# A decoder layer on one core: every product and difference of two tensors moved from GpSimd to VectorE

## The chip, the cores and the metric

The kernel runs on 1 core of one Trainium2 chip. The metric is device time in microseconds (us) of one execution, lower is better. The engines are named as in the profile: PE is TensorE (matmuls), DVE is VectorE, ACT is ScalarE, POOL is GpSimd, and SP issues most of the transfers. Each engine works through its own queue of instructions in order.

## The reference

One layer over 1024 tokens of width 1024, all in float32:

```python
x = x + 0.5 * swiglu(rmsnorm(x, g1), w_gate1, w_up1, w_down1)      # hidden width 2816
h = rmsnorm(x, g_mix)
qa, ka, va, qkv_b, beta, decay, gdn_gate, gate_a, gate_b = split(h @ w_in)
# branch A: rotary on qa and ka, causal dilated window attention in 3 groups of 4 heads (64 wide),
#           groups merged by a softmax over their log-denominators
# branch B: short causal convolution and silu on q, k, v; gated DeltaNet in chunks,
#           8 heads of 128; rmsnorm of the result times silu(gdn_gate)
x = x + (sigmoid(gate_a) * (A @ w_branch_a) + sigmoid(gate_b) * (B @ w_branch_b)) @ w_out
x = x + 0.5 * swiglu(rmsnorm(x, g2), w_gate2, w_up2, w_down2)
return rmsnorm(x, g_final)

def rmsnorm(x, g):  return x * rsqrt(mean(x * x) + 1e-6) * g
def rope(x1, x2):   return concat(x1 * cos - x2 * sin, x2 * cos + x1 * sin)
```

## The kernel before

Every large float32 product is made of three matmuls on parts of its operands. An operand is split in two: the high part `fH` is a cast that ACT makes, and the low part `fL` is the difference between the operand and `fH`. For weights this is `ff_split`, on 128x512 pieces of the raw tile `fraw` that SP's queue loads. Its difference (L222) runs on DVE, except in the mixer, where the flag `C.pool_split` sends it to POOL. Three matmuls per step of 128 then go to PE (L161 for projections of the mixer and merge, L279 and L409 in the hidden layers, L589 in the down projections).

The program has these stages. (1) Norm of the eight input tiles and the first matmuls. (2) The hidden layer of the first feed-forward part and its down projection, at whose end `done1` makes the norm for the mixer, tile by tile; `First` then makes the values of the first attention group and PE's banks for them are copied out by ACT (L809). (3) The mixer, first attention: for each of six pairs of heads, two rotary tiles (`rope_tile`) and eight blocks. (4) The mixer, eight DeltaNet heads: `gdn_keys`, `gdn_inverse` (a triangular solve of 62 short dependent DVE steps, L1041 to L1047, then a merge on PE), `gdn_values`, `gdn_scan` (eight steps in which PE and DVE take turns; `R` L1192, `v` L1200). Projections of later heads and of the gates fill PE in between. (5) The merge of the branches with the next norm, (6) the second feed-forward part, and `done2` with the final norm.

The norm of a tile is in `make_h`: the square sum on ACT (L186), the reciprocal root on DVE in 12 small steps (`rsqrt_cols`, L123 to L130), the product with the gain, transposes on PE (L206) and a split of the result. On even input tiles DVE makes one instruction of gain and root (L196). On all other tiles POOL multiplies with the gain (L198) and ACT scales by the root (L200). `done2` does the same on POOL (L1493), with half of the scaling on ACT (L1495) and half on DVE (L1497).

In `rope_tile`, ACT's queue issues four transfers that swap the halves of a tile (L836); then DVE multiplies the tile with the cosine (L837), POOL the swapped one with the sine (L838), and DVE adds (L840, L845 or L848). In `gdn_keys`, POOL scales the keys by a factor per token (L1139).

The order on each engine is made by a list scheduler that goes by priorities. Inside the mixer each piece of code stands in a `band`: attention first, then head 0, head 1 and so on, and the projections (`bulk`, with their weight splits) last. A change of the engine of an instruction thus changes the order around it too. The weight ring holds nine `fH` and nine `fL` pieces and two raw tiles.

Of the kernel before, what the change touches and what calls it, by code (L numbers as in the profile page):

```python
# [133 lines left out]
def load_w(C, *parts):  # L134

    nc = C.nc
    raw = C.wp.tile([P, 2048], F32, name="fraw", tag="fraw", bufs=2)
    for view, src in parts:
        nc.sync.dma_start(view(raw), src)
    return [ff_split(C, raw[:, q * 512:q * 512 + 512], eng=nc.gpsimd if C.pool_split else None) for q in range(2)]  # L140


def load_w2(C, src):
# [43 lines left out]
    return rsqrt_cols(C, ssq, 1.0 / D, EPS, 1, "rn")[0]  # L187


def make_h(C, x_t, t, gB, pool, bufs, on_dve=False):  # L190

    nc = C.nc
    xs = row(C, pool, "xg", "xg", bufs)
    if on_dve:
        r = rstd(C, x_t, pool)
        nc.vector.scalar_tensor_tensor(xs, x_t, r, gB, op0=ALU.mult, op1=ALU.mult)  # L196
    else:
        nc.gpsimd.tensor_tensor(out=xs, in0=x_t, in1=gB, op=ALU.mult)  # L198
        r = rstd(C, x_t, pool)
        nc.scalar.activation(xs, xs, AF.Copy, scale=r)  # L200

    def turn():
        for q in range(2):
            ps = psum(C, "tA")
            for f in range(4):
                nc.tensor.transpose(ps[:, f * P:f * P + P], xs[:, (q * 4 + f) * P:(q * 4 + f) * P + P], C.ident)  # L206
            v = ps.rearrange("p (f t) -> p f t", t=P)
            split_to(C, C.hH[:, q * 4:q * 4 + 4, t * P:t * P + P], C.hL[:, q * 4:q * 4 + 4, t * P:t * P + P], v)

    return turn  # L210


def ff_split(C, src, n=512, eng=None):

    nc = C.nc
    H = C.wp.tile([P, 512], F32R, name="fH", tag="fH", bufs=9)
    L = C.wp.tile([P, 512], F32R, name="fL", tag="fL", bufs=9)
    h, l = H[:, :n], L[:, :n]
    if len(src.shape) == 3:
        h, l = [v.rearrange("p (k n) -> p k n", n=src.shape[2]) for v in (h, l)]  # L220
    nc.scalar.copy(h, src)  # L221
    (eng or nc.vector).tensor_tensor(out=l, in0=src, in1=h.bitcast(F32), op=ALU.subtract)  # L222
    return H, L


# [599 lines left out]
def rope_tile(C, w_in, c0, g):  # L825

    nc = C.nc
    raw, sw, out = t4(C, "xp")[:, :T], t4(C, "vb")[:, :T], t4(C, "ka")[:, :T]
    with band(C, "bulk"):
        W = load_w2(C, cols(w_in, c0))  # L830
        for a in (0, 1):
            ps = proj(C, W, a, "mm")
            nc.scalar.copy(raw[:, a * 512:a * 512 + 512], ps)
    with band(C, "att"):
        for b in range(4):
            nc.scalar.dma_start(sw[b * 32:b * 32 + 32, :], raw[(b ^ 1) * 32:(b ^ 1) * 32 + 32, :])  # L836
        nc.vector.tensor_tensor(out=raw, in0=raw, in1=C.cosT, op=ALU.mult)  # L837
        nc.gpsimd.tensor_tensor(out=sw, in0=sw, in1=C.sinT, op=ALU.mult)  # L838
        if g == 0:
            nc.vector.tensor_tensor(out=out, in0=raw, in1=sw, op=ALU.add)  # L840
        elif g == 1:
            for n in range(2):
                o = out.rearrange("p (r n i) -> p r n i", r=4, n=2)[:, :, n]
                a, b = [v[:, n * 512:n * 512 + 512].rearrange("p (i r) -> p r i", r=4) for v in (raw, sw)]
                nc.vector.tensor_tensor(out=o, in0=a, in1=b, op=ALU.add)  # L845
        else:
            a, b = [v.rearrange("p (i r) -> p r i", r=8) for v in (raw, sw)]
            nc.vector.tensor_tensor(out=out.rearrange("p (r i) -> p r i", r=8), in0=a, in1=b, op=ALU.add)  # L848
    return out
# [253 lines left out]
def gdn_keys(C, w_in, h, Dm):  # L1103

    nc = C.nc
    X = Head()
    X.h = h
    with band(C, f"h{h}"):
        ssq = C.gd.tile([P, 16], F32, name="gssq", tag="gssq", bufs=2)
        X.k = t4c(C, "ka")  # L1110
        gdn_conv(C, w_in, C_KB + h * P, 8 + h, X.k)
        X.kd = t4c(C, "ka")
        ssq_tokens(C, X.k, X.kd, ssq[:, 0:8])
        X.q = t4c(C, "ka")
        gdn_conv(C, w_in, C_QB + h * P, h, X.q)
        ssq_tokens(C, X.q, None, ssq[:, 8:16])
        rs, sv = rsqrt_cols(C, ssq, 1.0, EPS, 16, "rg")
        cl = C.gd.tile([P, 5, NT], F32, name="cl", tag="cl", bufs=2)
        s, X.nk, ks, X.so = cl[:, 0], cl[:, 1], cl[:, 2], cl[:, 3]
        ns = cl[:, 4]  # L1120
        nc.vector.tensor_tensor(out=s, in0=rs[:, 0:8], in1=rs[:, 0:8], op=ALU.mult)
        nc.vector.tensor_tensor(out=s, in0=s, in1=C.beta[:, :, h], op=ALU.mult)
        nc.vector.tensor_tensor(out=X.nk, in0=rs[:, 0:8], in1=sv[:, 0:8], op=ALU.mult)
        nc.vector.tensor_tensor(out=ks, in0=s, in1=C.eS[:, :, h], op=ALU.mult)
        nc.vector.tensor_scalar(X.so, rs[:, 8:16], float(P) ** -0.5, None, op0=ALU.mult)
        nc.vector.tensor_scalar(ns, s, -1.0, None, op0=ALU.mult)

        X.N, X.A = t4c(C, "ka"), t4c(C, "ka")
        for src, dst, sc in ((X.k, X.N, ns), (X.q, X.A, s)):
            for q in range(2):  # L1130
                ps = psum(C, "tA")
                for i in range(4):
                    c = q * 4 + i
                    nc.tensor.matmul(ps[:, i * P:i * P + P], X.k[:, c, :], src[:, c, :], start=True, stop=True)
                for i in range(4):
                    c = q * 4 + i
                    nc.vector.scalar_tensor_tensor(dst[:, c, :], ps[:, i * P:i * P + P], sc[:, c:c + 1], Dm[:, c, :],
                                                   op0=ALU.mult, op1=ALU.mult)
        nc.gpsimd.tensor_tensor(out=X.kd, in0=X.kd, in1=ks.unsqueeze(2).to_broadcast([P, NT, P]), op=ALU.mult)  # L1139
    return X  # L1140


# [262 lines left out]
def open_pools(C, tc, st):  # L1405
    C.nc = tc.nc
    C.tc = tc
    C.pool_split = False
    C.fx = None
    C.cp = st.enter_context(tc.tile_pool(name="cp", bufs=1))  # L1410
    C.hp = st.enter_context(tc.tile_pool(name="hp", bufs=1, reuse_waits="tile"))
    C.tp = st.enter_context(tc.tile_pool(name="tp", bufs=2))
    C.pp = st.enter_context(tc.tile_pool(name="pp", bufs=1, space=bass.MemoryType.PSUM))
    C.dp = st.enter_context(tc.tile_pool(name="dp", bufs=1, space=bass.MemoryType.DRAM))
    C.hH, C.hL = Quarters(), Quarters()
    for th in (0, 1):
        new_h(C, th)
    C.x1d = C.dp.tile([T, D], F32, name="x1d")
    C.x2d = C.dp.tile([T, D], F32, name="x2d")
    C.hd = {n: [C.dp.tile([P, 512], F32, name=f"hd{n}x{p}") for p in range(NPAIR)] for n in range(1, 8)}  # L1420
    C.od = [C.dp.tile([T, 2, 132], F32, name=f"od{g}") for g in range(3)]
    C.vd = [C.dp.tile([T, 256], F32, name=f"vd{g}") for g in (1, 2)]
    C.v0d = C.dp.tile([T, 272], F32, name="v0d")
    C.yad = C.dp.tile([P, 2, T], F32, name="yad")
    C.sgad = [C.dp.tile([P, T], F32, name=f"sgad{f}") for f in range(8)]
    C.sgbd = [C.dp.tile([P, T], F32, name=f"sgbd{f}") for f in range(8)]
    C.ybd = [C.dp.tile([P, T], F32, name=f"ybd{f}") for f in range(8)]
    C.nbd = [C.dp.tile([32, 1024], F32, name=f"nbd{f}") for f in range(2)]
    C.ud = [C.dp.tile([32, 1024], F32, name=f"ud{f}") for f in range(2)]


def layer(tc, I, out):
# [6 lines left out]
    with ExitStack() as st:  # L1439
# [3 lines left out]
        with pool("s1") as sp:  # L1443
# [4 lines left out]
            for t in range(NT):  # L1448
                if t:
                    nc.sync.dma_start(xs[t], I["x"][t * P:t * P + P])  # L1450
                make_h(C, xs[t], t, gB, sp, 8, t % 2 == 0)()
                if t == 1:
                    W = [ff_tiles(C, I[w], 0) for w in ("ffn1_w_gate", "ffn1_w_up")]
        with pool("fx") as C.fx:
# [22 lines left out]
            first.blocks(range(4, NT))  # L1477
        C.fx = None
        with pool("ms") as C.ms:
            C.pool_split = True  # L1480
            mixer(C, tc, I)
            C.pool_split = False
        with pool("fx2") as C.fx:
            gB2 = load_gain(C, I["ffn2_norm"])
            first = merge_out(C, tc, I, gB2)
# [4 lines left out]

            def done2(t, x):
                y = row(C, C.fx, "y", None, None)
                nc.gpsimd.tensor_tensor(out=y, in0=x, in1=gF, op=ALU.mult)  # L1493
                r = rstd(C, x, C.fx)
                nc.scalar.activation(y[:, :512], y[:, :512], AF.Copy, scale=r)  # L1495
                nc.sync.dma_start(out[t * P:t * P + P, :512], y[:, :512])
                nc.vector.tensor_scalar(y[:, 512:], y[:, 512:], r, None, op0=ALU.mult)  # L1497
                nc.sync.dma_start(out[t * P:t * P + P, 512:], y[:, 512:])

            ff_down(C, C.x2d, down, done2)  # L1500

# [25 lines left out]
```

## Time and profile before

| | |
|---|---|
| time, median of 3 runs | 2700.59 us (2696.6 to 2703.91) |
| time of the profiled execution | 2714.74 us |
| its span | 2713.0 us |
| busy PE, DVE, ACT, POOL | 2576.8, 1793.9, 1003.0, 317.8 us |
| POOL's products and differences | splits 173.7, rotary 34.6, norms 20.0 + 19.9 + 19.4 + 11.4, keys 15.2 us |
| granted PE clock, mean | 0.969 |

In rows of groups the columns are line, engine, operation, output and inputs, shapes, count, then busy time in us and mean of one in ns, then the idle time of the engine before them and what ended it. In a timeline, a row has the start and the length in us. In a list of waits, the first is who waited, behind the arrow who was waited for, then us in total, times, and the longest.

### The profile page before, as it was taken

The numbers are of one execution on the slowest core, as the hardware profiler recorded it, in microseconds if no ns is written. First come the engines' busy times: TensorE is split into PE (matmuls) and PEld (weight loads), VectorE is DVE, ScalarE is ACT, GpSimd is POOL, SyncE is SP. The second block draws the span as 40 slices with busy tenths as digits, with TensorE's granted clock in tenths as the row PEclk, the third lists the DMA queues.
The fourth block names the chain that finished last, engine by engine and source line by source line (L and its number), as shares of the span: only waits on it lengthen the run. The fifth ranks groups of instructions, "written<-read, shape, count | busy, mean of one in ns | idle before, by whom it ended". The sixth has DMA issues, their size and how long they took to land.

```text
span 2713.0 us, 35365 instructions
## 1 busy us (share of the span) xinstructions
PE 2576.8 (95%) x12739; PEld 2111.5 (78%) x12739; DVE 1793.9 (66%) x3923; ACT 1003.0 (37%) x1857; POOL 317.8 (12%) x236
## 2 busy tenths in 40 slices
PE   7999999999899999899999999899999999999996
PEld 6888888887777867777777777777778888888885
DVE  8866666678342335878787875635647866667677
ACT  5333333445332324423333333225434333333444
POOL 1000000002322232212122211200101000000002
PEclk9999999999988989999999998999999999999998
DMA  4322337553423222312112211225442332238452
GB/s 156 109 91 107 105 113 258 162 176 132 126 58 82 80 75 69 102 53 61 46 44 68 57 49 47 74 103 200 169 160 89 106 109 103 100 110 289 132 190 78
DMA packets 258174, 301.07 MB, mean 111 GB/s; under 512 B 41840, under 2 KB 175184, under 8 KB 258000
## 3 DMA queue, kind: packets, MB, share of 16 engines
q1 hardware_dynamic: 255696, 292.54, 32.9%
q10 hardware_dynamic: 2304, 6.29, 1.0%
q8 instruction: 100, 1.64, 0.2%
q14 instruction: 74, 0.61, 0.1%
HBM read 217.34 MB, written 75.14 MB: 108 GB/s over the span
## 4 chain that ended last, share of the span: by engine, by line
PE 43%; DVE 13%; DMA 1%; ACT 1%; issue 1%; SPq 0%; ACTq 0%; DVEq 0%
PE mm L161 10%; PE tC L409 6%; PE mm L409 4%; PE tM L409 4%; DVE fsP L1046 2%; PE mm L589 2%; PE tC L589 2%; PE tM L589 2%; PE tA L589 2%; PE tC L1386 2%; DVE fsP L1041 1%; PE mm L1386 1%; PE tC L161 1%; DVE fsT L1047 1%; DVE ka L970 1%
## 5 line engine op out<-in xcount | busy, mean ns | idle before, releaser
L221 ACT CAST fH<-fraw 128x512 fp32r<-128x512 f32 x482 | 295.2, 620 | 650.9 <-PE mm L161 190.6
L161 PE MATMUL mm<-hH,fL 128*128 128x512 f32 x1024 | 422.8, 413 | 0.0
L161 PE MATMUL mm<-hH,fH 128*128 128x512 f32 x1024 | 419.5, 410 | 0.0
L161 PE MATMUL mm<-hL,fH 128*128 128x512 f32 x1024 | 419.3, 409 | 0.0
L222 DVE TENSOR_TENSOR fL<-fraw,fH 128x512 fp32r<-128x512 f32 x354 | 246.4, 700 | 103.8 <-ACT fH L221 102.8
L222 POOL TENSOR_TENSOR fL<-fraw,fH 128x512 fp32r<-128x512 f32 x128 | 173.7, 1360 | 589.2 <-ACT fH L221 494.2
L161 PEld LDWEIGHTS mm<-hH,fL 128*128 128x128 f32 x1024 | 199.4, 195 | 37.5 <-issue 1.3
L161 PEld LDWEIGHTS mm<-hL,fH 128*128 128x128 f32 x1024 | 198.6, 194 | 38.0 <-issue 2.3
L161 PEld LDWEIGHTS mm<-hH,fH 128*128 128x128 f32 x1024 | 198.5, 194 | 37.0 <-issue 1.9
L409 PE MATMUL mm<-hH,fH 128*128 128x512 f32 x320 | 124.5, 389 | 0.0
L409 PE MATMUL mm<-hL,fH 128*128 128x512 f32 x320 | 124.5, 389 | 0.0
L409 PE MATMUL mm<-hH,fL 128*128 128x512 f32 x320 | 124.5, 389 | 0.0
L582 DVE TENSOR_TENSOR hid<-hid,fH 128x512 fp32r<-128x512 f32 x154 | 106.3, 691 | 4.8 <-ACT fH L581 4.8
L581 ACT CAST fH<-hid 128x512 fp32r<-128x512 f32 x154 | 94.8, 616 | 18.2 <-PE tM L409 6.6
L1493 POOL TENSOR_TENSOR y<-acc,gB 128x1024 f32<-128x1024 f32 x8 | 19.4, 2439 | 630.6 <-DVE acc L624 624.0
L970 DVE SCALAR_TENSOR_TENSOR ka<-xp,cw,ka 128x512 f32<-128x512 f32 x96 | 82.1, 857 | 15.4 <-ACT ka L968 13.9
L198 POOL TENSOR_TENSOR xg<-acc,gB 128x1024 f32<-128x1024 f32 x8 | 19.9, 2506 | 616.1 <-DVE acc L624 610.5
L221 ACT CAST fH<-hH 128x512 fp32r<-128x512 f32 x68 | 42.4, 623 | 101.9 <-PE tC L589 50.3
L222 DVE TENSOR_TENSOR fL<-hH,fH 128x512 fp32r<-128x512 f32 x68 | 49.1, 722 | 46.8 <-ACT fH L221 46.8
L589 PE MATMUL mm<-fL,fH 128*128 128x512 f32 x176 | 69.7, 396 | 4.5 <-DVE fL L222 4.5
L837 DVE TENSOR_TENSOR xp<-xp,U 128x1024 f32<-128x1024 f32 x12 | 17.0, 1420 | 82.8 <-DMA vb<-xp 82.8
L409 PEld LDWEIGHTS mm<-hL,fH 128*128 128x128 f32 x320 | 60.1, 188 | 12.6
(401 smaller groups left out, 6393.3 us busy)
## 6 DMA issues: line engine op xcount, KB each, us to landing
fraw<-in_w_in_dram SPq DMA_DIRECT2D x66, 512.0 KB, 3.7
fraw<-in_ffn_w_gate_dram SPq DMA_DIRECT2D x22, 1024.0 KB, 5.1
fraw<-in_ffn_w_up_dram SPq DMA_DIRECT2D x22, 1024.0 KB, 5.4
hL<-in_ffn_w_down_dram SPq DMA_DIRECT2D x8, 1024.0 KB, 6.6
fraw<-in_ffn_w_down_dram SPq DMA_DIRECT2D x8, 1024.0 KB, 6.3
fraw<-in_w_branch_b_dram SPq DMA_DIRECT2D x8, 1024.0 KB, 5.1
fraw<-in_w_out_dram SPq DMA_DIRECT2D x8, 1024.0 KB, 7.8
vb<-xp ACTq DMA_DIRECT2D x48, 128.0 KB, 2.4
```

The source lines that it names most:

```text
L161: nc.tensor.matmul(ps, w, x, start=k == 0 and i == 0, stop=k == kt - 1 and i == 2)
L221: nc.scalar.copy(h, src)
L222: (eng or nc.vector).tensor_tensor(out=l, in0=src, in1=h.bitcast(F32), op=ALU.subtract)
L409: nc.tensor.matmul(ps, w, x, start=opens and k == 0 and q == 0, stop=k == 3 and q == 2, skip_group_check=True)
L581: C.nc.scalar.copy(h, v.bitcast(F32))
L582: C.nc.vector.tensor_tensor(out=v, in0=v.bitcast(F32), in1=h.bitcast(F32), op=ALU.subtract)
L589: self.C.nc.tensor.matmul(ps, x[:, m], w, start=p == 0 and i == 0, stop=p == NPAIR - 1 and i == 2)
L970: nc.vector.scalar_tensor_tensor(o, x, w, o, op0=ALU.mult, op1=ALU.add)
L1041: nc.vector.tensor_tensor(out=v, in0=Th[:, :, :, 0:n], in1=mv, op=ALU.mult)
L1046: nc.vector.tensor_tensor(out=v, in0=Tx[:, 0:4, 0:n], in1=mv, op=ALU.mult)
L1047: nc.vector.tensor_reduce(out=Tx[:, 0:4, i], in_=v, axis=AX.X, op=ALU.add)
L1386: nc.tensor.matmul(ps, mx[:, c], W[k][w], start=i == 0, stop=i == len(seq) - 1)
```

## The change

All of POOL's operations on two tensors go to DVE. `ff_split` has no choice of engine any more; the second rotary product and the key scaling change their engine alone; and the norms use one DVE instruction for gain and root on every tile, so that ACT's scaling goes away too. In `done2` this instruction runs on two halves of the tile, each stored when it is done. POOL keeps memsets, one copy and the masking of the decay.

```diff
 def load_w(C, *parts):
-    return [ff_split(C, raw[:, q * 512:q * 512 + 512], eng=nc.gpsimd if C.pool_split else None) for q in range(2)]
+    return [ff_split(C, raw[:, q * 512:q * 512 + 512]) for q in range(2)]

-def make_h(C, x_t, t, gB, pool, bufs, on_dve=False):
+def make_h(C, x_t, t, gB, pool, bufs):
     xs = row(C, pool, "xg", "xg", bufs)
-    if on_dve:
-        r = rstd(C, x_t, pool)
-        nc.vector.scalar_tensor_tensor(xs, x_t, r, gB, op0=ALU.mult, op1=ALU.mult)
-    else:
-        nc.gpsimd.tensor_tensor(out=xs, in0=x_t, in1=gB, op=ALU.mult)
-        r = rstd(C, x_t, pool)
-        nc.scalar.activation(xs, xs, AF.Copy, scale=r)
+    r = rstd(C, x_t, pool)
+    nc.vector.scalar_tensor_tensor(xs, x_t, r, gB, op0=ALU.mult, op1=ALU.mult)

 def ff_split(...):
     nc.scalar.copy(h, src)
-    (eng or nc.vector).tensor_tensor(out=l, in0=src, in1=h.bitcast(F32), op=ALU.subtract)
+    nc.vector.tensor_tensor(out=l, in0=src, in1=h.bitcast(F32), op=ALU.subtract)

 def rope_tile(...):
-        nc.gpsimd.tensor_tensor(out=sw, in0=sw, in1=C.sinT, op=ALU.mult)
+        nc.vector.tensor_tensor(out=sw, in0=sw, in1=C.sinT, op=ALU.mult)

 def gdn_keys(...):
-        nc.gpsimd.tensor_tensor(out=X.kd, in0=X.kd, in1=ks.unsqueeze(2).to_broadcast([P, NT, P]), op=ALU.mult)
+        nc.vector.tensor_tensor(out=X.kd, in0=X.kd, in1=ks.unsqueeze(2).to_broadcast([P, NT, P]), op=ALU.mult)

 def done2(t, x):
-                nc.gpsimd.tensor_tensor(out=y, in0=x, in1=gF, op=ALU.mult)
                 r = rstd(C, x, C.fx)
-                nc.scalar.activation(y[:, :512], y[:, :512], AF.Copy, scale=r)
-                nc.sync.dma_start(out[t * P:t * P + P, :512], y[:, :512])
-                nc.vector.tensor_scalar(y[:, 512:], y[:, 512:], r, None, op0=ALU.mult)
-                nc.sync.dma_start(out[t * P:t * P + P, 512:], y[:, 512:])
+                for h in (slice(0, 512), slice(512, 1024)):
+                    nc.vector.scalar_tensor_tensor(y[:, h], x[:, h], r, gF[:, h], op0=ALU.mult, op1=ALU.mult)
+                    nc.sync.dma_start(out[t * P:t * P + P, h], y[:, h])
```

Lines of the changed kernel are a few less: the split L222 is L217 there, the solve's L1041 and L1042 are L1036 and L1037, the key scaling L1139 is L1134, ACT's copy L809 is L804.

Three places of the new order. First DVE's queue inside the triangular solve of the fifth head. `fsP` and `fsT` are the solve's, `seg` a part of the next head's decay, `vT` a convolution, `vb` the head's values. Before:

```order
L1041 TENSOR_TENSOR fsP<-fsT,Tm 128x104
L996 TENSOR_TENSOR seg<-masks,gH 128x512
L1042 TENSOR_REDUCE fsT<-fsP 128x2x4
L996 TENSOR_TENSOR seg<-masks,gL 128x512
L1041 TENSOR_TENSOR fsP<-fsT,Tm 128x112
```

and now, some steps earlier in the same solve:

```order
L1155 TENSOR_TENSOR vb<-tA,cl 128x512
L1036 TENSOR_TENSOR fsP<-fsT,Tm 128x24
L217 TENSOR_TENSOR fL<-fraw,fH 128x512
L1037 TENSOR_REDUCE fsT<-fsP 128x2x4
L965 SCALAR_TENSOR_TENSOR vT<-xp,cw,vT 128x512
L1036 TENSOR_TENSOR fsP<-fsT,Tm 128x32
```

Work of other parts stood between a product of the solve and its sum already; now splits stand there too. This solve has five of them, where it had none; two more stand between its end and the step that takes its result (`Tm`), one right behind that step, and two at the end of the scan.

Second, DVE's queue in the scan of the same head. `R`, `v`, `S` are the scan's, `cl` are the factors of the next head's keys, and `ka` in L1137 (now L1132) its key products. Before:

```order
L1122 TENSOR_TENSOR cl<-cl,beta 128x8
L1125 TENSOR_SCALAR cl<-rgy 128x8
L1124 TENSOR_TENSOR cl<-cl,ex 128x8
L1126 TENSOR_SCALAR cl<-cl 128x8
L1192 SCALAR_TENSOR_TENSOR R<-tC,neG,vb 128x128
L1137 SCALAR_TENSOR_TENSOR ka<-tA,cl,Dm 128x128 x2
L1200 COPY v_13337<-tC 128x128
```

and now:

```order
L1117 TENSOR_TENSOR cl<-cl,beta 128x8
L1119 TENSOR_TENSOR cl<-cl,ex 128x8
L1121 TENSOR_SCALAR cl<-cl 128x8
L1134 TENSOR_TENSOR ka<-ka,cl 128x1024
L1195 COPY v_13268<-tC 128x128
L1132 SCALAR_TENSOR_TENSOR ka<-tA,cl,Dm 128x128 x2
L1203 SCALAR_TENSOR_TENSOR S<-S,ex,tC 128x128
```

The key scaling (L1134) stands between the `R` and the `v` of one scan step, with the factors; it was on POOL.

Third, ACT's queue at the end of the first down projection. `sq` is the square sum of a finished tile `acc`, `xg` the normalised tile, `rny` its root from DVE, `vs` the copy of a bank that PE needs again. Before (with the buffers' numbers):

```order
L186 ACTIVATE sq_5836,ssq_5837<-acc_4856 128x1024
L221 CAST fH_6287<-fraw_6281 128x512
L200 ACTIVATE xg_5799<-xg_5799,rny_5805 128x1024
L809 COPY vs_5880<-tM_5855 128x272
L221 CAST fH_6559<-fraw_6557 128x512
L200 ACTIVATE xg_5834<-xg_5834,rny_5840 128x1024
```

and now:

```order
L186 ACTIVATE sq_5790,ssq_5791<-acc_4850 128x1024
L804 COPY vs_5868<-tM_5843 128x272
L216 CAST fH_6547<-fraw_6545 128x512
L216 CAST fH_6551<-fraw_6545 128x512
L804 COPY vs_5896<-tM_5871 128x272
L186 ACTIVATE sq_5824,ssq_5825<-acc_4852 128x1024
```

ACT's copy of the bank no longer stands behind scalings that wait for DVE's root; it stands behind square sums, which wait for finished tiles.

More of the change, by code (lines that the diff above doesn't have):

```diff
@@ L210, in make_h, with ff_split @@
     return turn
-def ff_split(C, src, n=512, eng=None):
+def ff_split(C, src, n=512):
     nc = C.nc
@@ L1407, in open_pools @@
     C.tc = tc
-    C.pool_split = False
     C.fx = None
@@ L1450, in layer @@
                     nc.sync.dma_start(xs[t], I["x"][t * P:t * P + P])
-                make_h(C, xs[t], t, gB, sp, 8, t % 2 == 0)()
+                make_h(C, xs[t], t, gB, sp, 8)()
                 if t == 1:
@@ L1479, in layer @@
         with pool("ms") as C.ms:
-            C.pool_split = True
             mixer(C, tc, I)
-            C.pool_split = False
         with pool("fx2") as C.fx:
```

## The prediction

> **What bounds the kernel now.** I read the page's costliest groups first, then the busy time by stage, then the timeline of VectorE (DVE) beside GpSimd (POOL), and last what TensorE (PE) waited for. The two groups that the change is mostly about, from the page:
>
> ```profile
> L222 DVE TENSOR_TENSOR fL<-fraw,fH 128x512 fp32r<-128x512 f32 x354 | 246.4, 700 | 103.8 <-ACT fH L221 102.8
> L222 POOL TENSOR_TENSOR fL<-fraw,fH 128x512 fp32r<-128x512 f32 x128 | 173.7, 1360 | 589.2 <-ACT fH L221 494.2
> ```
>
> One split of a weight tile costs 0.70 us on DVE and 1.36 on POOL, which is idle most of the time. By that alone the change loads the busier engine. The stages (columns: stretch, its length, then busy time and instruction count of PE, PE's weight loads, DVE, ACT, POOL, then granted clock, DMA share, GB/s):
>
> ```profile
> 0.00:50.00 50.00, 33.43 (x238) 31.69 (x239) 38.56 (x128) 30.52 (x49) 11.58 (x8) 0.97 0.53 191
> 600.00:715.00 115.00, 102.07 (x546) 88.89 (x545) 85.19 (x180) 57.19 (x99) 32.14 (x18) 0.94 0.38 124
> 715.00:1080.00 365.00, 346.79 (x1819) 274.89 (x1818) 138.56 (x391) 123.75 (x359) 92.53 (x60) 0.93 0.30 81
> 1080.00:1800.00 720.00, 669.65 (x3867) 539.36 (x3867) 538.84 (x1519) 241.12 (x426) 142.08 (x134) 0.95 0.22 60
> ...
> 2650.00:2713.00 63.00, 41.93 (x172) 33.82 (x170) 48.00 (x136) 26.15 (x45) 19.40 (x8) 0.86 0.21 77
> ```
>
> POOL works in five places: the first norm (0 to 50), the end of the first feed-forward part (600 to 715), attention (715 to 1080), the DeltaNet heads (1080 to 1800), and merge and final norm. In the hidden parts PE is always busy and POOL idle, so nothing happens there. In the heads DVE is busy 75% of the time with serial work, and PE follows it.
>
> What decides is what POOL does to DVE. From the timeline of the end (start, length, engine):
>
> ```profile
> 2692.73 2.40 POOL L1493 TENSOR_TENSOR y<-acc,gB 128x1024 f32<-128x1024 f32 x1 [1.17 <-DVE rny L130]
> 2692.86 2.29 DVE L129 SCALAR_TENSOR_TENSOR rnt<-rnt,rnv 128x1 f32<-128x1 f32 x1
> ```
>
> An operation on one element per partition lasts 2.29 us and ends with the POOL product that started just before it. The line's own view (min/median/max) of a sister operation, and a DVE group in one head that reads one operand from PSUM:
>
> ```profile
> L126 DVE CUSTOM_DVE_ANT_0 rny<-rny,magic x32: 145/159/2365, 6.4 to 2707.0; 128x2 uint16<-128x2 uint16 x32
> L1137 DVE SCALAR_TENSOR_TENSOR ka<-tA,cl,Dm 128x128 f32<-128x128 f32 x16 | 4.9, 342 | 0.0
> ```
>
> 0.16 is the normal price, 2.37 the price under a POOL product; the L1137 group keeps to 0.34. So POOL's products of two tensors stop DVE instructions that read two tensors from SBUF. [...]
>
> **The change part by part.** DVE gains 128 splits at 0.70 (90 us; 9 stand before 715, 40 in attention, 79 in the heads), 12 rotary and 8 key products at 1.23 (25), 20 norm products at 1.28 (26), and eight output tiles in two halves. POOL loses all of its products, ACT 20 scalings by the root and 8 of the output. What that does is different in each stage.
>
> *Start.* The rows of DVE and PE, and the price of the norm product on DVE:
>
> ```profile
> 17.29 2.11 DVE L222 TENSOR_TENSOR fL<-fraw,fH 128x512 fp32r<-128x512 f32 x1
> 19.92 6.84 DVE L222 TENSOR_TENSOR fL<-fraw,fH 128x512 fp32r<-128x512 f32 x5
> 25.02 0.39 PE L279 MATMUL tC<-hH,fL 128*128 128x256 f32 x1 [3.16 <-DVE fL L222]
> L196 DVE SCALAR_TENSOR_TENSOR xg<-xin,rny,gB x4: 1276/1278/1284, 8.3 to 39.6; 128x1024 f32<-128x1024 f32 x4
> ```
>
> Six splits took 8.95 us where 6 x 0.70 = 4.2 are due, and PE waited 3.16 for them. DVE pays 4 x 1.28 = 5.1 for the products of the odd tiles, mostly later, while PE has matmuls queued. I take -3 (ends: 0, if those products come in front of the splits, and -5).
>
> *End of the first down projection.* Here POOL, DVE and ACT stand in one chain:
>
> ```profile
> 638.92 2.90 DVE L222 TENSOR_TENSOR fL<-hH,fH 128x512 fp32r<-128x512 f32 x1
> ...
> PE tA L206 <- ACT xg L200: 4.3, 1, 4.3
> PE tM L806 <- ACT vs L809: 7.8, 1, 7.8
> ...
> 687.47 1.15 ACT L200 ACTIVATE xg<-xg,rny 128x1024 f32<-128x1024 f32 x1 [3.69 <-DVE rnv L123]
> ```
>
> The first wait is for the first normalised tile, whose root was held up on DVE by POOL. In the second PE needs a bank that ACT should have copied out; ACT stood at L200, waiting for the root. The change takes L200 out of ACT's queue and the stretches out of DVE's: both waits go, -12. The products that DVE takes over (8 x 1.28) are shorter than what POOL costs it there; late next is the first tile's square and root. Ends: -4, if DVE's own queue is late by as much, and -16, with the slow matmuls after each wait.
>
> *Attention.* Rotary: both products wait for the same transfer; POOL's is the longer one (first two rows), and PE waits for the sum (window 715 to 1080):
>
> ```profile
> L838 POOL TENSOR_TENSOR vb<-vb,Tm x12: 2355/2866/3442, 736.8 to 1013.2; 128x1024 f32<-128x1024 f32 x12
> L837 DVE TENSOR_TENSOR xp<-xp,U x12: 1215/1226/2104, 734.5 to 1013.2; 128x1024 f32<-128x1024 f32 x12
> ...
> PE tC L869 <- DVE ka L845: 5.1, 2, 4.3
> PE tC L869 <- DVE ka L848: 4.8, 1, 4.8
> PE tC L869 <- DVE ka L840: 2.7, 2, 2.6
> ```
>
> Before, the sum starts 2.87 after the transfer, now 2 x 1.23 = 2.45 if both products come after it. A split that stands ahead on POOL (1.36) no longer delays the product, and nothing stops the sum: 0.4 + 1.36 = 1.8 at best. I take 1.6 for each of the five waits: -8 (ends 0 and all 12.6). The 40 splits cost 28 us on an engine that is idle for 226 of 365: nothing, as long as each finds its ACT copy made.
>
> *Heads.* The DVE groups of one head (window 1440 to 1527), stretched ones with unstretched neighbours:
>
> ```profile
> L970 DVE SCALAR_TENSOR_TENSOR ka<-xp,cw,ka 128x512 f32<-128x512 f32 x12 | 9.9, 824 | 3.1 <-ACT ka L968 2.9
> L970 DVE SCALAR_TENSOR_TENSOR vT<-xp,cw,vT 128x512 f32<-128x512 f32 x6 | 4.5, 748 | 2.5 <-ACT vT L968 2.5
> L1041 DVE TENSOR_TENSOR fsP<-fsT,Tm 128x128 f32<-128x128 f32 x1 | 1.5, 1517 | 0.0
> L1046 DVE TENSOR_TENSOR fsP<-fsT,Tm 128x124 f32<-128x124 f32 x1 | 1.4, 1356 | 0.0
> L125 DVE TENSOR_SCALAR roy<-rov 128x8 int32<-128x8 int32 x1 | 1.1, 1105 | 0.0
> L1046 DVE TENSOR_TENSOR fsP<-fsT,Tm 128x76 f32<-128x76 f32 x1 | 1.1, 1093 | 0.0
> L1041 DVE TENSOR_TENSOR fsP<-fsT,Tm 128x16 f32<-128x16 f32 x1 | 1.1, 1081 | 0.0
> L1046 DVE TENSOR_TENSOR fsP<-fsT,Tm 128x128 f32<-128x128 f32 x1 | 0.4, 399 | 0.0
> L1041 DVE TENSOR_TENSOR fsP<-fsT,Tm 128x24 f32<-128x24 f32 x1 | 0.2, 189 | 0.0
> ```
>
> The four stretched steps of the triangular solve lose 1.12 + 0.96 + 0.69 + 0.89 = 3.7 against 0.40, 0.40, 0.40 and 0.19; the convolution 12 x 0.076 = 0.9, the root 0.9: 5.5 us a head, all on DVE's serial path. Into it come 79/8, about 10 splits (7.0) and the key product (1.2): 8.2. In the new order five splits stand inside the solve, where DVE waits for nothing: paid, 3.5. The key product stands in the scan between two steps that PE waits for: paid, 1.2. The other five stand where DVE has waits anyway:
>
> ```profile
> DVE vT L970 <- ACT vT L968: 5.0, 2, 2.5
> ...
> DVE ka L970 <- ACT ka L968: 2.9, 2, 2.3
> ```
>
> So 4.7 - 5.5 = -0.8 a head, -6 for eight. Ends: none paid, -44; all paid, and each split waiting for ACT's copy as the 354 on DVE do now (103.8/354 = 0.29), 8.2 + 2.9 - 5.5 = +5.6 a head, +45. I take a value near the middle, since the order shows half of the splits on each side. Queued behind a split that waits are the solve and the scan, and PE behind them. The weight loads wait on SP's queue for the splits to free the raw tile:
>
> ```profile
> SPq L139 <- POOL fL L222: 382.7, 54, 27.2
> ```
>
> They run far ahead of PE, so an earlier release by half a microsecond costs and gains nothing.
>
> *Merge and end.* One stretch stands in front of the second half's gates; at the end PE waits once for a split behind stretched operations, and two stretches follow its last matmul:
>
> ```profile
> 1952.66 2.36 DVE L129 SCALAR_TENSOR_TENSOR rnt<-rnt,rnv 128x1 f32<-128x1 f32 x1
> ...
> 2671.88 0.80 PE L589 MATMUL mm<-fL,fH 128*128 128x512 f32 x1 [4.49 <-DVE fL L222]
> ...
> 2698.05 2.20 DVE L128 TENSOR_TENSOR rnt<-rny 128x1 f32<-128x1 f32 x1
> ...
> 2703.15 2.20 DVE L128 TENSOR_TENSOR rnt<-rny 128x1 f32<-128x1 f32 x1
> ```
>
> Merge: -2 (0 to -6). End: PE's wait of 4.49 goes, and after the last matmul the two stretches of 2.2. Each of the last three tiles pays half a product (1.28/2 = 0.64) more on DVE: -4.5 - 4.4 + 1.9 = -7 (ends -2 and -9).
>
> Sum: -3 - 12 - 8 - 6 - 2 - 7 = -38. The profiled execution's span is 2713.0, its time 2714.74, 14 above the median of the runs shown, 2700.59; the profiled 2714.74 would become 2677, the median 2663.
>
> **The rivals.** *DVE becomes the bound in the heads, and the kernel slower.* For it: DVE 538.84 of 720 there, 8.2 us more a head, in-order waits for ACT. Against: the stretches go, and DVE still has waits to fill. At +45 in the heads the sum is 2700.6 - 32 + 45 = 2714; it turns to slower when a head loses more than 4 us. [...]
> *About no change:* the heads lose some 4 us each and eat the rest, 2700.
> *Hidden gain:* attention and heads give nothing, since PE's projections fill what comes free; start, projection, merge and end stay: -24, 2677.
> *None of the splits is paid:* heads -44, in all -76, 2625.
>
> **How the numbers follow.** Forecast (2640 to 2690) 0.48, hidden gain 0.20, none paid 0.14, no change 0.08, slower 0.10. A change under 0.3% (8 us) can't be told from none. Faster 0.48 + 0.20 + 0.14 = 0.82, same 0.08, slower 0.10. The range runs from the case that nothing is paid to that of no change, 2622 to 2698; slower and the tails stay out.
>
> **What would show it.** No 128x1 operation on DVE over 1 us; PE without the waits of 4.3, 7.8, 3.16 and 4.49; solve steps of 0.2 to 0.4 with splits of 0.7 between them; POOL busy under 30 us. I am wrong if DVE stands before L217 for ACT's copies by more than 0.4 us each in the heads, or if the new order leaves PE short of projections there.

## The result, and the profile after

The changed kernel takes 2586.45 us (median, 2583.77 to 2594.1) against 2700.95 for the kernel before in the same job: a ratio of 0.958, 95% interval 0.956 to 0.961. The gain is 114 us where 38 were forecast; the time lies below the range. The profiled execution has a span of 2584.5 us against 2713.0, 128.5 less; the stages below are told in spans. The profiled execution of the kernel before lies 14 us above that kernel's median, so about 14 of the 128.5 belong to that execution and not to the change.

The page of the changed kernel, its row of busy times and the group of all weight splits (columns as in the prediction):

```profile
PE 2527.0 (98%) x12739; PEld 2077.2 (80%) x12739; DVE 1807.6 (70%) x4099; ACT 977.3 (38%) x1829; POOL 24.4 (1%) x60
...
L217 DVE TENSOR_TENSOR fL<-fraw,fH 128x512 fp32r<-128x512 f32 x482 | 328.9, 687 | 173.2 <-ACT fH L216 171.6
```

DVE does 176 instructions more and is busy only 13.7 us more (1793.9 before). PE does the same 12739 matmuls, in 49.8 us less of busy time (2576.8 before): it ran them faster, which the prediction had priced at one place only. The trace also lists the stretches in which PE was granted half its clock, called half-clock records or spells below: 168.4 us in all before, 46.4 now. The rest of the 128.5, 78.7 us, is idle time of PE that went.

By stage (length, busy and count of PE, weight loads, DVE, ACT, POOL, then granted clock). The heads lie at 1049 to 1727 now, and lay at 1116 to 1834:

```profile
0.00:50.00 50.00, 37.68 (x274) 36.16 (x275) 41.22 (x142) 28.61 (x49) 0.20 (x4) 1.00 0.56 202
600.00:715.00 115.00, 113.15 (x615) 97.24 (x614) 88.90 (x221) 55.02 (x99) 0.95 (x1) 1.00 0.47 150
715.00:1080.00 365.00, 359.84 (x1966) 287.92 (x1965) 197.99 (x583) 139.00 (x388) 4.89 (x12) 1.00 0.31 85
...
1049.00:1727.00 678.00, 653.27 (x3866) 527.23 (x3864) 523.72 (x1543) 240.66 (x425) 20.27 (x47) 0.98 0.24 68
```

The granted clock is 1.00 in the first three, which had 0.97, 0.94 and 0.93. In the heads PE is idle for 678.0 - 653.3 = 24.7 us; here is the same stretch of the kernel before, and what PE waited for in it:

```profile
1116.00:1834.00 718.00, 662.44 (x3823) 534.45 (x3821) 516.79 (x1430) 235.19 (x412) 133.37 (x128) 0.95 0.21 60
```
```profile
PE tA L980 <- ACT ka L971: 14.1, 6, 3.6
PE tC L1231 <- DVE vb L1227: 8.7, 6, 2.5
PE tA L1159 <- ACT vT L971: 8.2, 7, 1.6
PE tM L1075 <- DVE Tm L1057: 7.1, 2, 3.9
PE tA L1134 <- DVE ka L1137: 6.3, 2, 3.6
```

Idle were 718.0 - 662.4 = 55.6 us, 31 more. The list of the changed kernel for its heads, its first and longest rows:

```profile
PE tA L975 <- ACT ka L966: 8.7, 6, 1.9
PE tC L1226 <- DVE vb L1222: 2.1, 5, 0.8
PE tM L1070 <- DVE Tm L1052: 1.4, 2, 1.3
```

Last the small operation of the norms, and DVE's groups in one steady head of the changed kernel (window 1363 to 1445):

```profile
L126 DVE CUSTOM_DVE_ANT_0 rny<-rny,magic x32: 148/159/161, 6.1 to 2578.2; 128x2 uint16<-128x2 uint16 x32
```
```profile
L965 DVE SCALAR_TENSOR_TENSOR ka<-xp,cw,ka 128x512 f32<-128x512 f32 x12 | 9.0, 746 | 1.3 <-ACT ka L963 1.1
L217 DVE TENSOR_TENSOR fL<-fraw,fH 128x512 fp32r<-128x512 f32 x10 | 6.8, 683 | 0.1
...
L1036 DVE TENSOR_TENSOR fsP<-fsT,Tm 128x128 f32<-128x128 f32 x1 | 0.4, 402 | 0.0
...
L1041 DVE TENSOR_TENSOR fsP<-fsT,Tm 128x124 f32<-128x124 f32 x1 | 0.4, 371 | 0.0
...
L1041 DVE TENSOR_TENSOR fsP<-fsT,Tm 128x76 f32<-128x76 f32 x1 | 0.4, 357 | 0.0
```

The largest value of L126 fell from 2.365 us to 0.161. The solve steps of 1.52, 1.36 and 1.09 us take 0.40, 0.37 and 0.36. Ten splits stand in the head, and DVE waits 0.1 us for their ACT copies, not the 0.29 each that the upper end of the heads' term feared.

### The profile page after: what moved, and what is told of

It reads as the page before. It is cut to its first block, busy times and chain, and to the rows that moved or that the text cites. A ratio compares the mean times of both kernels' runs of the same rounds, so it can differ in the third digit from the quotient of the medians.

```text
span 2584.5 us, 35226 instructions
## 1 busy us (share of the span) xinstructions
PE 2527.0 (98%) x12739; PEld 2077.2 (80%) x12739; DVE 1807.6 (70%) x4099; ACT 977.3 (38%) x1829; POOL 24.4 (1%) x60
## 4 chain that ended last, share of the span: by engine, by line
PE 80%; DVE 13%; DMA 2%; ACT 2%; issue 2%; SPq 0%; DVEq 0%; ACTq 0%
PE mm L161 16%; PE tC L404 13%; PE mm L404 8%; PE tM L404 8%; PE tC L584 4%; PE mm L584 4%; PE tA L584 3%; PE tM L584 3%; PE mm L274 2%; PE tC L274 2%; PE tC L1381 2%; PE mm L697 2%; PE mm L1381 2%; DVE fsP L1041 1%; PE tC L864 1%
## 5 line engine op out<-in xcount | busy, mean ns | idle before, releaser
L217 DVE TENSOR_TENSOR fL<-fraw,fH 128x512 fp32r<-128x512 f32 x482 | 328.9, 687 | 173.2 <-ACT fH L216 171.6
L161 PE MATMUL mm<-hH,fL 128*128 128x512 f32 x1024 | 413.7, 404 | 0.0
L161 PE MATMUL mm<-hH,fH 128*128 128x512 f32 x1024 | 413.0, 403 | 0.7 <-ACT xp L955 0.7
L161 PE MATMUL mm<-hL,fH 128*128 128x512 f32 x1024 | 411.4, 402 | 0.0
L161 PEld LDWEIGHTS mm<-hH,fH 128*128 128x128 f32 x1024 | 194.7, 190 | 37.6 <-ACT xp L955 1.1
L161 PEld LDWEIGHTS mm<-hH,fL 128*128 128x128 f32 x1024 | 194.6, 190 | 36.5 <-issue 1.0
L404 PE MATMUL mm<-hH,fH 128*128 128x512 f32 x320 | 124.5, 389 | 0.0
L404 PE MATMUL mm<-hL,fH 128*128 128x512 f32 x320 | 124.5, 389 | 0.0
L404 PE MATMUL mm<-hH,fL 128*128 128x512 f32 x320 | 124.5, 389 | 0.0
L965 DVE SCALAR_TENSOR_TENSOR ka<-xp,cw,ka 128x512 f32<-128x512 f32 x96 | 72.2, 753 | 11.7 <-ACT ka L963 10.8
L217 DVE TENSOR_TENSOR fL<-hH,fH 128x512 fp32r<-128x512 f32 x68 | 46.9, 690 | 41.3 <-ACT fH L216 41.3
L404 PEld LDWEIGHTS mm<-hL,fH 128*128 128x128 f32 x320 | 60.1, 188 | 12.6
L404 PEld LDWEIGHTS mm<-hH,fL 128*128 128x128 f32 x320 | 60.1, 188 | 12.5
L404 PEld LDWEIGHTS mm<-hH,fH 128*128 128x128 f32 x320 | 60.1, 188 | 12.4
L584 PE MATMUL mm<-fH 128*128 128x512 f32 x176 | 68.6, 390 | 0.0
L584 PE MATMUL tC<-fH 128*128 128x512 f32 x176 | 68.6, 390 | 0.0
L584 PE MATMUL tC<-fH,hid 128*128 128x512 f32 x176 | 68.5, 389 | 0.0
```

Of the source, the lines that this page charges most:

```text
L161: nc.tensor.matmul(ps, w, x, start=k == 0 and i == 0, stop=k == kt - 1 and i == 2)
L217: nc.vector.tensor_tensor(out=l, in0=src, in1=h.bitcast(F32), op=ALU.subtract)
L404: nc.tensor.matmul(ps, w, x, start=opens and k == 0 and q == 0, stop=k == 3 and q == 2, skip_group_check=True)
L584: self.C.nc.tensor.matmul(ps, x[:, m], w, start=p == 0 and i == 0, stop=p == NPAIR - 1 and i == 2)
L965: nc.vector.scalar_tensor_tensor(o, x, w, o, op0=ALU.mult, op1=ALU.add)
```

## The experiments

The theory: a product of two tensors on POOL stops DVE's instructions that read two SBUF tensors (a 128x1 operation took 2.29 us under a product of 2.40); PE then waits, and behind such waits it runs at half the clock for a while (records of 13.65 us behind the waits of 2.6, 4.3 and 4.8 in the attention blocks of the kernel before). Rivals: the other order, or POOL's lateness, made the time; or PE's waits cost only themselves. Each ratio is to the kernel before in the same job. Gains by stage come from the start of the first matmul of each stage (of the first solve step on DVE for the heads). The diffs are shortened: flags that limit an edit to the mixer, and repeated lines, are left out.

### One part undone at a time

```diff
# u_split: the mixer's 128 splits on POOL again
-    nc.vector.tensor_tensor(out=l, in0=src, in1=h.bitcast(F32), op=ALU.subtract)
+    (eng or nc.vector).tensor_tensor(out=l, in0=src, in1=h.bitcast(F32), op=ALU.subtract)
# u_rope: 12 sine products
-        nc.vector.tensor_tensor(out=sw, in0=sw, in1=C.sinT, op=ALU.mult)
+        nc.gpsimd.tensor_tensor(out=sw, in0=sw, in1=C.sinT, op=ALU.mult)
# u_keys: 8 key scalings
-        nc.vector.tensor_tensor(out=X.kd, in0=X.kd, in1=ks...
+        nc.gpsimd.tensor_tensor(out=X.kd, in0=X.kd, in1=ks...
# u_norm: make_h and done2 as in the kernel before
```

> The changed kernel with the mixer's 119 to 128 weight splits back on POOL, all else as changed. Lock theory (POOL's products of two tensors stop DVE, PE then waits and its clock drops): most of the mixer's gain goes back, +40 to +70 us against the changed kernel (2625 to 2655), DVE groups of the solve stretched again to over 1 us, half-clock spells of PE back in the heads. Rival, latency theory (what counted was how long the rotary and norm products took on POOL, not that DVE stood still): the splits run far ahead of PE, so 0 to +10 us, or even a gain, since DVE is relieved of 88 us of work.

Measured: 2645.55 us, ratio 0.978 (0.975 to 0.981), span 2640.7, 56 longer than the changed kernel's: 39 of it in the heads, 11 between the last attention block and the first solve. Half-clock records in the heads grow from 29 to 59 us.

> The changed kernel with only the twelve rotary sine products back on POOL. Lock theory: 12 products of 2.4 to 2.9 us hold DVE's own cosine product up, some +5 to +15 us, all in attention. Latency theory: attention's whole gain of some 47 us hangs on the rotary chain in front of PE, so +25 to +45 us and PE's half-clock spells of 13 us at each group are back.

Measured: 2589.81 us, ratio 0.957 (0.955 to 0.960), span 2586.1: nothing, so neither theory's figure came.

> The changed kernel with only the eight key scalings back on POOL. Lock theory: each takes 1.2 us off DVE's scan but stops DVE for up to 1.9: -5 to +10 us. Latency theory: the scaled keys are needed a head later, DVE is relieved: -10 to 0 us.

Measured: 2584.25 us, ratio 0.955 (0.952 to 0.957), span 2580.2: nothing that this run can tell; it is taken up again below.

> The changed kernel with the norms as before (POOL multiplies with the gain, ACT scales by the root, done2 as before), all else as changed. Both theories: +30 to +45 us: start 6, end of the first down projection 16, merge 12, end 10 (stage differences of the two profiles). If much less, the gains at these places came from the order around them.

Measured: 2615.44 us, ratio 0.966 (0.964 to 0.969), span 2613.0, 28.5 longer: 5.6 in the start, 13.2 from the end of the first feed-forward part to the first attention block, 5.7 in the merge, 8.8 at the end, less 4.9 in the mixer. That is a little under the 30 to 45 expected: the merge gave back 5.7 where 12 were thought. What PE waited for up to 760 us is back with it:

```profile
PE tA L206 <- DVE xg L196: 9.2, 1, 9.2
PE tA L206 <- ACT xg L200: 7.6, 2, 4.3
PE tM L806 <- ACT vs L809: 6.0, 1, 6.0
PE tC L279 <- DVE fL L222: 3.1, 1, 3.1
```

The last three hold the waits of 4.3, 7.8 (6.0 here) and 3.16 that the prediction named; the first (for the first tile of all) stands in the changed kernel too. So the norms are worth 28 us and the splits 56, but 28 + 56 + 2 - 4 = 82 is far from 128.5: some parts act together.

### Two parts together

```diff
# u_split_rope: u_split and u_rope in one kernel
```

> The mixer's 128 splits and the 12 rotary sine products go back to POOL together, all else as changed. Each alone cost 0.020 (splits) and nothing (rotary). Theory (POOL's products stop DVE, PE then waits at the rotary sums, and each such wait of 4 to 5 us costs PE another spell of half clock): in attention the two add more than the sum of each, since the sine product queues behind a split on POOL; the waits of 4 to 5 us before the first block of a group return, with three or four half-clock records of 10 to 14 us between 700 and 1080 us; ratio 0.985 to 0.992. Rival (the parts are independent): ratio 0.977, no long half-clock record in attention.

Measured: 2674.81 us, ratio 0.988 (0.986 to 0.990), span 2674.6, 90 longer than the changed kernel's. In the attention blocks u_split loses nothing, u_rope 4.6, both together 28.0; the kernel before loses 28.3 there. Windows from the first attention block to the last, of the kernel before, of u_split and of u_split_rope:

```profile
753.00:1040.00 287.00, 273.67 (x1480) 215.83 (x1480) 101.03 (x305) 90.17 (x299) 68.20 (x41) 0.92 0.27 72
```
```profile
737.00:995.00 258.00, 257.19 (x1480) 205.72 (x1479) 108.81 (x315) 90.22 (x299) 46.98 (x32) 0.99 0.29 80
```
```profile
738.00:1025.00 287.00, 273.49 (x1480) 216.04 (x1482) 101.09 (x305) 90.25 (x299) 68.19 (x41) 0.92 0.27 72
```

Read the second and third column: from u_split to u_split_rope the same 1480 matmuls take 16.3 us more of busy time (273.5 for 257.2), at a clock of 0.92 for 0.99, and PE is idle for 13.5 us where it was for 0.8. Idle are the waits for the rotary sum, which are those of the kernel before to a tenth:

```profile
PE tC L864 <- DVE ka L840: 5.1, 2, 4.3
PE tC L864 <- DVE ka L843: 4.8, 1, 4.8
PE tC L864 <- DVE ka L835: 2.7, 2, 2.6
```

The clock records of the trace have three spells of 13.65 us at half clock, at 737, 850 and 963, each beginning in the last microsecond of such a wait. With u_split, and in the changed kernel, PE does not wait for these sums by more than 0.2 us, and no such spell stands there (u_split has one record of 3.41 us in its blocks, the changed kernel none). A fourth record of u_split_rope, 6.83 us at 1010, has no wait above 1.5 us ahead of it. POOL and DVE ahead of the wait that ends at 850.8:

```profile
844.06 1.29 POOL L217 TENSOR_TENSOR fL<-fraw,fH 128x512 fp32r<-128x512 f32 x1 [5.99 <-ACT fH L216]
845.30 3.33 POOL L833 TENSOR_TENSOR vb<-vb,Tm 128x1024 f32<-128x1024 f32 x1
...
848.66 3.10 DVE L840 TENSOR_TENSOR ka<-xp,vb 128x512 f32<-128x512 f32 x2 [2.23 <-POOL vb L833]
```

The sine product queues behind a split and then takes 3.33 us, where six of the twelve of the kernel before took 2.35 to 2.40, while DVE's cosine product runs. The two halves of the sum take 3.10 us with the next split beside them, where 2.1 (1.07 each in the changed kernel) are due. Together that makes the sum just late enough for PE to run dry.

### The lock by itself

```diff
# d_read: behind each split of the mixer, on POOL (scr is a tile of its own)
+        nc.gpsimd.tensor_copy(C.scr[:, 0:1], h[:, 0:1])
+        nc.gpsimd.tensor_tensor(out=C.scr, in0=C.scr, in1=C.scr, op=ALU.mult)
# d_write: the same, with writes alone
+        nc.gpsimd.tensor_copy(C.scr[:, 0:1], h[:, 0:1])
+        for _ in range(3):
+            nc.gpsimd.memset(C.scr, 0.0)
```

> The changed kernel, and after each of the mixer's splits POOL also does a product of its own of two SBUF tensors, 128x512, whose result nobody uses. The orders on PE, DVE and ACT stay as changed. Theory (a POOL product of two SBUF tensors stops DVE while it runs): the stretched DVE operations come back, 50 to 100 us slower than the changed kernel, ratio 0.977 to 0.995. Rival (what the splits on POOL cost was their own lateness and the other order, not the lock): ratio 0.958, within 0.3% of the changed kernel.

> As the run with POOL's own products, but POOL does three memsets of 128x512 in their place, which read nothing and write as much each. The orders on PE, DVE and ACT are those of the changed kernel. Theory (only a POOL instruction that reads SBUF stops DVE): ratio 0.956 to 0.961, no stretched DVE operations. Rival (any work of POOL stops DVE): ratio 0.977 to 0.995, as with the products.

Measured: d_read 2640.43 us, ratio 0.976 (0.974 to 0.978), span 2637.7; d_write 2588.13 us, ratio 0.956 (0.954 to 0.959), span 2583.0. POOL's groups and a DVE line (min/median/max) of d_read, then of d_write:

```profile
L220 POOL TENSOR_TENSOR scr<-scr 128x512 f32<-128x512 f32 x128 | 158.7, 1240 | 10.3 <-POOL scr L219 0.2
...
L968 DVE SCALAR_TENSOR_TENSOR vT<-xp,cw,vT x48: 717/744/1491, 1077.4 to 1671.4; 128x512 f32<-128x512 f32 x48
```
```profile
L221 POOL MEMSET scr<- 128x512 f32 x384 | 202.2, 527 | 22.1
...
L969 DVE SCALAR_TENSOR_TENSOR vT<-xp,cw,vT x48: 712/745/754, 1063.3 to 1621.4; 128x512 f32<-128x512 f32 x48
```

Nobody waits for this work of POOL, and DVE still does all its splits. The orders on PE, DVE and ACT are those of the changed kernel, in d_read apart from some places before 763 us. With 159 us of POOL products the span is 53 us longer, 42 of it in the heads, and the longest of the 48 DVE operations above takes 1.49 us; with 202 us of POOL writes, which fill POOL's queue more, the span is the changed kernel's and the longest takes 0.75. That is the lock, shown: it costs about as much as sending the splits to POOL (56), so for the splits neither the order nor POOL's lateness is what counted.

### What half clock costs

```diff
# d_rope: four more DVE products per rotary tile, ahead of the sum
+        for _ in range(4):
+            nc.vector.tensor_tensor(out=sw, in0=sw, in1=sw, op=ALU.max)
# w_split_rope (on u_split_rope) and w_after (on the changed kernel):
# three matmuls after the cosine product of each group's first key tile
+            ps = psum(C, "tC")
+            for _ in range(3):
+                nc.tensor.matmul(ps, C.ident, raw[:, :512], start=True, stop=True)
```

> The changed kernel, and DVE does four more products of 128x1024 (maximum of the swapped tile with itself, about 1.23 us each) between the sine product and the sum of each of the 12 rotary tiles: the sum comes 4.9 us later, POOL has no part in it. Theory (a PE wait of 4 to 5 us costs a half-clock spell beside itself): waits of 3 to 5 us before the first block of a group, with half-clock records of 10 to 14 us behind them; 15 to 40 us slower than the changed kernel, ratio 0.964 to 0.973. Rival A (a wait costs only itself): waits return without the records, +8 to +15, ratio 0.961 to 0.964. Rival B (PE has projections to fill it): ratio 0.958.

Measured: 2614.56 us, ratio 0.967 (0.964 to 0.969). It decides less than hoped: the scheduler moved some 650 of PE's 12739 matmuls, the longest waits for the three kinds of sum are 3.3, 1.9 and 0.9 us, and the attention blocks have records of 3.41, 3.41, 3.41 and 17.07 us. The time is the one that the theory gave, but the waits are shorter than it said, and the profiled execution (2603.35 us) is the fastest of the four.

> The run with splits and rotary on POOL (ratio 0.9881), and PE does three more float32 matmuls of 128x512 into a bank that is overwritten, just before the first block of each of the three groups, where it waits for the rotary sum; they need only the cosine product, which is earlier. The sum comes as late as before, but PE idles less ahead of it. Theory (the half-clock spell comes from PE's idling and costs time of its own): the three records of 13.65 us go or shrink, attention gets 10 to 20 us shorter though PE has more to do, ratio 0.981 to 0.985. Rival (what PE loses there is the wait alone, or the spell has another cause): records stay, ratio 0.987 to 0.992.

> The changed kernel with the same nine matmuls at the same places, where PE hardly waits for the sum. It prices the fill: nine times some 0.9 us, 4 to 10 us slower than the changed kernel, ratio 0.958 to 0.961, and no record in attention.

Measured: w_split_rope 2662.65 us, ratio 0.985 (0.983 to 0.987), against 0.988 (0.986 to 0.990) without the useless matmuls; span 12.3 shorter (2662.3 for 2674.6), 12.0 of it in the attention blocks. The two intervals touch, and by the ratios the gain is some 9 us; the traces below carry the reading. w_after 2591.35 us, ratio 0.959 (0.956 to 0.961), 2.4 us longer in span than the changed kernel: less than the 4 to 10 expected and within the noise. PE's timeline at the first group, of u_split_rope and then of w_split_rope:

```profile
737.93 0.80 PE L864 MATMUL tC<-ka 64*128 64x128 f32 x4 [2.57 <-DVE ka L835]
738.66 0.79 PE L161 MATMUL mm<-hL,fH 128*128 128x512 f32 x1
739.25 0.63 PE L161 MATMUL mm<-hH,fL 128*128 128x512 f32 x1
739.81 1.23 PE L864 MATMUL tC<-ka 64*128 64x256 f32 x4
```
```profile
733.26 2.74 PE L836 MATMUL tC<-xp,ident 128*128 128x512 f32 x6
737.31 0.49 PE L868 MATMUL tC<-ka 64*128 64x128 f32 x4 [1.31 <-DVE ka L839]
737.73 0.50 PE L161 MATMUL mm<-hL,fH 128*128 128x512 f32 x1
738.07 0.40 PE L161 MATMUL mm<-hH,fL 128*128 128x512 f32 x1
738.39 0.70 PE L868 MATMUL tC<-ka 64*128 64x256 f32 x4
```

The sum comes about as late in both. In the first PE idles 2.57 us and the same instructions then take 0.80, 0.79, 0.63 and 1.23; in the second it works for 2.74 of that time, idles 1.31, and they take 0.49, 0.50, 0.40 and 0.70. The three records of 13.65 are gone. One of 10.24 at 994 stands 2 us behind a wait of 2.8 us, which got no extra matmuls. So these spells come from idling, and they cost their own time: with 8.2 us more of matmuls (nine, 0.91 each) the span is 12 us shorter. In the kernel before every record but the last, which runs on past the end, is 3.41, 6.83, 10.24, 13.65 or 17.07 us long, multiples of the shortest. The one at 737.3 of u_split_rope began 2.0 us after the last matmul, inside the wait of 2.57.

### What the splits and the key scaling cost on DVE now

```diff
# n_split: no difference for the mixer's weights
-    nc.vector.tensor_tensor(out=l, in0=src, in1=h.bitcast(F32), op=ALU.subtract)
-    return H, L
+    return H, H
# v_keys_pool: as u_keys;  v_keys_act:
-        nc.vector.tensor_tensor(out=X.kd, in0=X.kd, in1=ks...
+        for c in range(NT):
+            nc.scalar.activation(X.kd[:, c, :], X.kd[:, c, :], AF.Copy, scale=ks[:, c:c + 1])
```

> The changed kernel once more, beside the versions below: ratio 0.956 to 0.960.

> The changed kernel without the mixer's 128 differences: the low part of these weights is left out and the high part stands in its place, with as many matmuls. It tells what the 0.70 us of each split costs on DVE now. The prediction's step (half of the ten splits of a head are paid, 3.5 us a head): 20 to 35 us faster than the changed kernel, ratio 0.945 to 0.951. Rival (none is paid, since DVE has waits enough and PE is the bound): within 5 us, ratio 0.956 to 0.960.

> The changed kernel with the eight key scalings on POOL again, to tell whether the 0.35% that it was ahead is real. If the key scaling between two steps of the scan is paid on DVE (1.2 us a head): 4 to 9 us faster than the changed kernel, ratio 0.953 to 0.956. If it is hidden: the same ratio as the changed kernel.

> The changed kernel with the key scaling on ACT, as eight scalings of 128x128 a head, so that neither DVE pays it nor POOL stops DVE. If the key scaling is paid on DVE: 4 to 10 us faster than the changed kernel and as fast as with POOL or faster, ratio 0.952 to 0.956. Rival: ACT's 64 short instructions stand before the casts and copies that PE and DVE wait for, within 3 us of the changed kernel or slower.

Measured, in one job: the changed kernel 2584.88 us, ratio 0.9562 (0.9549 to 0.9575); n_split 2573.57, 0.952 (0.950 to 0.954); v_keys_pool 2585.7, 0.9561 (0.9547 to 0.9574); v_keys_act 2580.37, 0.9541 (0.9528 to 0.9554). The key scaling on POOL is worth nothing, so what u_keys seemed to be ahead was noise. On ACT it is some 5 us ahead, less than a measurement of this kernel can tell from no change. The 128 splits cost 11 us, about 0.09 each of the 0.69 that each lasts: neither half of them, as the prediction had it, nor quite none. The stages do not tell where: against the changed kernel of this job the attention blocks are 5.9 us shorter, the stretch up to the first solve 9.1 longer and the heads 11.5 shorter, and some 20 matmuls moved from the heads into that stretch. If all of the 11 lay in the heads it would be 1.4 a head.

## Why the prediction was wrong in size

The direction and the mechanism were right: POOL's products stopped DVE (2.37 us for an operation of 0.16), and taking them away paid although DVE got more to do. What failed is the price: the slow matmuls behind PE's waits were counted at one place and put at nothing everywhere else (PE's busy time fell by 49.8 us for the same matmuls), and the splits were charged to DVE's path in the heads at three times what they cost. The terms, in us of span:

| stage | predicted (ends) | measured |
|---|---|---|
| start | -3 (0 to -5) | -6.2 |
| end of the first down projection, to the first block | -12 (-4 to -16) | -14.5 |
| attention blocks | -8 (0 to -12.6) | -28.3 |
| from the last block to the first solve | no term | -18.5 |
| heads | -6 (-44 to +45) | -39.3 |
| merge | -2 (0 to -6) | -12.1 |
| end | -7 (-9 to -2) | -9.6 |
| sum | -38 | -128.5 |

*Start, first projection, end.* Right in mechanism, a little small; start and end lie just outside their ends. The named waits went, u_norm brings them back, and the product on DVE costs less than the stretches. In the start a half-clock record of 3.41 us stood behind the wait of 3.16, which the term left out. In the first projection the end of -16, "with the slow matmuls after each wait", was the better value.

*Attention: the step that failed is the bound "all 12.6".* Waits of 12.6 us were there and went whole, but they were taken for the most that could be gained. Behind them stood 16.3 us of slower matmuls. The prediction's own row for 715 to 1080 says it, granted clock 0.93; it was quoted for POOL's work and not priced. Slow matmuls after a wait were counted at one place, the first projection, and not carried over. The 1.6 us assumed for each wait was also too little: a split ahead of the sine product plus a stopped sum held PE for 4.3 and 4.8.

*From the last block to the first solve.* No term at all, and most of it is no gain of its own. The rows of the kernel before, then of the changed one:

```profile
1040.00:1116.00 76.00, 71.21 (x343) 56.56 (x344) 49.60 (x151) 33.92 (x67) 18.95 (x17) 1.00 0.41 115
```
```profile
991.00:1049.00 58.00, 57.44 (x283) 46.31 (x284) 40.17 (x130) 27.91 (x54) 1.77 (x5) 1.00 0.31 86
```

Of the 18 us some 14 are busy time of 60 matmuls that the new order puts elsewhere, 43 of them in the heads; 4 are idle time of PE that went. The clock was 1.00 in both.

*Heads: the share of splits that is paid.* Ten splits and a key product a head, half of the one and all of the other, made 4.7 us; n_split and v_keys_pool give at most 1.4 and 0. Undo that, and what the stretches had cost comes to 39 + 11 = 50 us, against the 44 (5.5 a head) of the prediction. That these are near is in part luck: the 44 counted stretched DVE rows alone, while in the 50 there are half-clock records (68 us before, 29 now), less the matmuls that moved in. The cost was set three times too high because a place in DVE's order was read as a price. PE is what ends the heads now: idle 24.7 of 678. In the fifth and sixth head the solve itself did become longer by its splits, 27.3 to 28.8 us, but the next head's solve begins 0.6 us behind this head's norm on DVE, where it took 8.3, and a head is 82 us long instead of 87.

*Merge.* One stretched step in front of the gates was priced. The list of waits of the kernel before has 7.9 us, in three waits, for the high parts `mH` of the merged values (PE L1386 on ACT L166), 0.4 now, and a half-clock spell of 10 us stood behind it. u_norm accounts for 5.7 of the 12.1; the rest stays open.

*Sum of the parts.* u_split_rope and u_norm give back 90.1 + 28.5 = 118.6 of 128.5, nearly all where each belongs. The remaining 10, of which 6 stand in the merge, was not pinned down; it is less than the 14 us by which the profiled execution of the kernel before lies above its median.

*The rivals.* DVE as the bound: refuted, the heads are 39 us shorter and DVE hardly waits for the splits' copies. Hidden gain: refuted, attention and heads gave most. "None of the splits is paid" came near in the heads (-44 against -39) and fell short in the other stages, by 20 us in the attention blocks alone.

## What to carry to other kernels

A second engine that takes products of two tensors off a busy DVE may take more from it than it gives, as the splits here did (56 us slower with them on POOL than on DVE): look at the largest duration of DVE's smallest operation, and if it is many times the median (2.365 us for 0.159 in the kernel before), price the offload by what PE waits for in every stage, not by the stretched rows of one head. Behind each wait of PE look at the granted clock of the same stage: with three waits of 2.6 to 4.8 us in the attention blocks came 16 us of slow matmuls. And an instruction that is added to an engine with waits to fill costs what its removal gains, which a run tells (0.09 of 0.69 us here), not its duration at its place in the order.

## What the runs showed of the hardware that was not expected

PE working on nothing can be faster than PE waiting: nine useless matmuls, 8.2 us, took 12 us off the span. In the trace of the kernel before, after its first 60 us, each of the 20 stretches of 2.0 us or more without a matmul has a half-clock record that begins in it or within 1.4 us of its end, or is running already; the five of 1.5 to 1.7 us have none. In the changed kernel three stretches of 1.9 us have one too. In u_split_rope and w_split_rope there are exceptions of up to 2.6 us. The spells behind those of the kernel before last 3.41 to 17.07 us; what sets the length stays open. And a long wait is not the only way in: with the sine products alone on POOL a record of 17 us stands at 873, where no listed wait for the sums is above 0.9 us; what set it off stays open too.

The stretch is not only for operations with two SBUF tensors, as the prediction put it: of DVE's scalar operations with one tensor (TENSOR_SCALAR) that started during a POOL product with 0.1 us or more of it left, 7 of 31 were stretched in the kernel before, the L125 row of 1.1 us among them. The seven have 2 or 8 elements per partition and began with 0.8 us or more of the product left; two others with more than one element had 0.1 us left; the 22 with one element per partition kept to 0.16 us, with up to 2.2 us left. None of 19 reductions was stretched, and none of 18 copies, but all of these copies read PSUM.
